# One transformer-like block on one core: the order of the first Strassen period and the way the first norm's gain reaches the core

## Chip, cores and metric

The kernel runs on 1 core of one Trainium2 chip. The metric is the device time of one execution in microseconds (us); the median of 3 runs of the kernel before is 1046.34 us (1046.23 to 1046.36).

## What is computed

One layer of a streaming encoder in float32, for 512 tokens of width 1024: a SwiGLU feed-forward (hidden width 2816) with half a residual, a mixer (chunked attention beside a convolution module, both gated), and a second SwiGLU feed-forward, each between two RMS norms.

```python
def rms_norm(x, g):
    y = x * lax.rsqrt(jnp.mean(x * x, axis=-1, keepdims=True) + EPS)
    return y * g

def swiglu(x, w_gate, w_up, w_down):
    return (jax.nn.silu(x @ w_gate) * (x @ w_up)) @ w_down

h = x
f = swiglu(rms_norm(h, ffn1_norm_pre), ffn1_w_gate, ffn1_w_up, ffn1_w_down)
h = h + 0.5 * rms_norm(f, ffn1_norm_post)
h = h + rms_norm(hybrid_mixer(rms_norm(h, mix_norm_pre), ...), mix_norm_post)
f = swiglu(rms_norm(h, ffn2_norm_pre), ffn2_w_gate, ffn2_w_up, ffn2_w_down)
h = h + 0.5 * rms_norm(f, ffn2_norm_post)
```

## The kernel before

Every product is made in float32 from two reduced-precision parts (`fp32r`) of each operand: a high part, which ScalarE (ACT) casts, and a low part, the rest, which VectorE (DVE) subtracts. `mm3` (lines 129 to 133) then issues three products to TensorE (PE): high by high, high by low, low by high.

**The start.** SP loads four tiles of `x` (128 tokens by 1024, 512 KB each) and weight blocks (`raw`, 512 KB each). The gain of the first norm has 1024 numbers; lines 268 to 271 load it with two DMAs of 256 KB, each of which writes the same 512 numbers to all 128 partitions. Meanwhile TensorE transposes the identity `WARM` times into a bank that nobody reads (lines 274 to 276). `stats1` sums squares on ACT and takes the root on GpSimd (POOL); `scaled1` (line 545) multiplies half a row of `h` by the root and the gain on DVE; `quarter` (line 558) transposes what came out on TensorE and ACT casts it into `uh`, the high part of the first feed-forward's input. On ACT the cast of the first weight block, `whi` (line 92), is written ahead of the four casts of `uh` (line 566). The first product is the matmul of line 196.

**The seven products.** Blocks 0 to 2 of the 22 hidden blocks of a feed-forward are made the plain way, blocks 3 to 21 (`CLASSIC = 3`) by Strassen's scheme, Winograd's form: seven half-size products in place of eight. The token sums s1 to s4 are made once; for each block j, four sums of weights are made on DVE: T1 and T3 in one tile `t13` (`sums13`, line 342), T2 and T4 in `t24` (`sums24`, line 349), T2 from T1. `parts(j, n)` makes the high part on ACT (line 363) and the low part on DVE (line 367) of the operand n: "b" (the gate block itself), "t13", "t24", "b22". `periods` (line 424) goes over j. In period j TensorE makes `first_products(j)` (b, t13 and t24, first halves), `third_products(j-1)` and `second_products(j)` (b and t13, second halves), 84 matmuls of 256 columns in all, while DVE and ACT prepare the operands of block j+1. Two small additions take products out of PSUM: `first_sum(j)` (line 417, a copy on ACT, of the first product's bank) and `second_sum(j)` (line 421, an addition on DVE, of the bank of the third of the first products). `second_products(j)` goes on accumulating in these two banks.

The feed-forward runs under `in_order()`, that is, each of TensorE, DVE and ACT works in the order in which the code is written. For the first period (j == j0, which is 3), `first_sum` and `second_sum` stand right behind `first_products` (lines 436 to 438), ahead of everything that prepares block 4. In later periods they stand between these steps. Tiles: `xn` (`wide`) has 3 buffers, `raw` 3, the pairs `whi`/`wlo` 6, PSUM 8 banks.

Of the kernel before, what the change touches and what calls it, by code (L numbers as in the profile page):

```python
# [8 lines left out]
F32 = mybir.dt.float32  # L9
# [3 lines left out]
ALU = mybir.AluOpType  # L13

P = 128
S = 512
D = 1024
# [21 lines left out]
C_ALL = C_LNB + NC  # L39

TAIL = 5
WARM = 36
AHEAD = 3
HALF = S // 2
CLASSIC = 3
# [7 lines left out]
def kernel(  # L53
# [11 lines left out]
    nc = tc.nc  # L65
# [4 lines left out]
    gpool = ctx.enter_context(tc.tile_pool(name="gpool", bufs=2))  # L70
# [9 lines left out]
    def bank():  # L80
        return psum.tile([P, 512], F32, name="ps")

    def two_banks():
        return [bank(), bank()]

    def wide():

        return tmps.tile([P, D], F32, name="xn")
# [17 lines left out]
    def pair_tiles():  # L106
        return ring.tile([P, 1024], F32R, name="whi"), ring.tile([P, 1024], F32R, name="wlo")
# [145 lines left out]
    ident = const.tile([P, P], F32, name="ident")  # L253
    make_identity(nc, ident)
    h = const.tile([P, NT, D], F32, name="h")
# [6 lines left out]
    def load_x(t):  # L262
        nc.sync.dma_start(out=h[:, t, :], in_=x[t * P:(t + 1) * P, :])

    load_x(0)
    load_x(1)

    g_first = gpool.tile([P, D], F32, name="gain")
    for b in range(2):
        sl = slice(b * 512, (b + 1) * 512)  # L270
        nc.sync.dma_start(out=g_first[:, sl], in_=gains[0, sl].partition_broadcast(P))
    with tc.manual_schedule(engines={mybir.EngineType.PE}):

        warm = bank()
        for _ in range(WARM):
            nc.tensor.transpose(warm[:, 0:P], ident, ident)
    ch = const.tile([P, C_ALL], F32, name="ch")
    tab_d = dram.tile([H, TABP], F32, name="tab_d")
# [44 lines left out]
    def seven_products(u, sums, hid, gu, j0, acts):  # L323
# [4 lines left out]
        s1, s2, s3, s4, _ = sums  # L328
# [9 lines left out]
        def add(out, a, b, op=ALU.add):  # L338
            nc.vector.tensor_tensor(out=out, in0=a, in1=b, op=op)  # L339
# [9 lines left out]
        def sums24(j):  # L349
            gate, up = raw[j]  # L350
            t24 = gu.tile([P, 1024], F32, name="t24")
            add(t24[:, lo], up[:, hi], ops[j]["t13"][1][:, lo], op=ALU.subtract)
            add(t24[:, hi], gate[:, hi], t24[:, lo], op=ALU.subtract)
            b22 = [gu.tile([P, 512], F32R, name=f"b22{p}", bufs=2) for p in "hl"]
            ops[j] |= {"t24": (pair_tiles(), t24), "b22": (b22, up[:, hi])}

        def parts(j, n):
            high(j, n)
            low(j, n)

        def high(j, n):
            (h_, _), src = ops[j][n]
            nc.scalar.copy(out=h_, in_=src)  # L363
# [53 lines left out]
        def first_sum(j):  # L417
            xs[j] = wide()
            nc.scalar.copy(out=xs[j][:, q[0]], in_=g[j][0][:, q[0]])

        def second_sum(j):
            add(xs[j][:, q[1]], g[j][1][:, q[0]], xs[j][:, q[0]])

        def periods():
            for j in range(j0, NF + 1):
                p, n = j - 1, j + 1
                old, now, new = p >= j0, j < NF, n < NF
                if old:
                    x, (g1, g2, g3) = xs[p], g[p]
                    y = ys[p] = wide()  # L430
                    add(x[:, q[2]], g2[:, q[0]], x[:, q[0]])
                    add(y[:, q[3]], g3[:, q[0]], x[:, q[2]])
                    silu(y[:, q[0]], g1[:, q[0]])
                if now:
                    first_products(j)
                if j == j0:
                    first_sum(j)
                    second_sum(j)
                if new:
                    sums13(n)  # L440
                    parts(n, "b")
                elif now:
                    prefetch(1)
                if now and j > j0:
                    first_sum(j)
                if new:
                    parts(n, "t13")
                elif now:
                    prefetch(2)
                if now and j > j0:  # L450
                    second_sum(j)
                if new:
                    sums24(n)
                if old:
                    third_products(p)
                    add(x[:, q[3]], g2[:, q[0]], x[:, q[0]])
                if new:
                    parts(n, "t24")
                elif now:
                    down_parts(2)  # L460
                if old:
                    silu(y[:, q[1]], x[:, q[3]])
                    add(y[:, q[2]], g3[:, q[0]], x[:, q[1]])
                    nc.vector.tensor_tensor(out=hid[:, p, :], in0=y[:, lo], in1=y[:, hi], op=ALU.mult)  # L464
                if new:
                    parts(n, "b22")
                load(j + 2)
                if now:
                    second_products(j)
# [75 lines left out]
    def scaled1(t, b):  # L545
        xn, r = xns[t]
        sl = slice(b * 512, (b + 1) * 512)
        nc.vector.scalar_tensor_tensor(xn[:, sl], h[:, t, sl], r, g_first[:, sl], op0=ALU.mult, op1=ALU.mult)

    def pre1(t):  # L550
        stats1(t)
# [475 lines left out]
```

## Time and profile before

| | |
|---|---|
| median of 3 runs | 1046.34 us (1046.23 to 1046.36) |
| the profiled execution, its own time | 1046.96 us |
| span in its profile | 1045.1 us |
| TensorE busy | 1030.9 us (99%) |
| DVE busy | 772.9 us (74%) |
| ACT busy | 476.0 us (46%) |
| mean granted clock of TensorE | 0.997 of full speed |

A busy time is the sum over an engine's instructions. Matmuls overlap: one of 256 columns is shown with 283 ns, and the next starts 120 ns behind it. What TensorE loses is therefore read from its idle times and from the distance of starts.

### The profile page before, as it was taken

What the parts mean: (1) busy time and instruction counts of PE and PEld (TensorE: products, weight loads), DVE (VectorE), ACT (ScalarE), POOL (GpSimd) and SP (SyncE); (2) the same over time, 40 slices, a digit from 0 to 9 for tenths busy, and PEclk for the clock granted to TensorE, in tenths of its full rate; (3) what the DMA queues carried; (4) which work ended last, traced back from release to release, by engine and by line L of the source; (5) the groups of instructions that cost most, each with busy time, mean ns of one, the idle gap of its engine ahead of it and who ended that gap; (6) DMA issues with size and microseconds to landing.
All of it is one profiled execution on the core that took longest, in us unless ns stands there. A gap on an engine that the chain in (4) does not pass through costs nothing.

```text
span 1045.1 us, 16111 instructions
## 1 busy us (share of the span) xinstructions
PE 1030.9 (99%) x6540; PEld 938.4 (90%) x6540; DVE 772.9 (74%) x1187; ACT 476.0 (46%) x785; POOL 20.7 (2%) x42
## 2 busy tenths in 40 slices
PE   8999999999999999999999999999999999999997
PEld 7999999998888898888888888899999999988886
DVE  6988898987332559999969776488889898963314
ACT  6434444445232432677874444354444444442311
POOL 1000000000000100000000100010000000000000
PEclk9999999999999999999999999999999999999999
DMA  7233333336323133333221145131334333452302
GB/s 245 64 100 110 101 114 102 101 102 220 101 88 96 41 112 109 121 96 97 82 87 61 41 132 169 43 101 41 103 101 121 100 104 102 127 177 88 95 20 81
DMA packets 30330, 106.92 MB, mean 102 GB/s; under 512 B 3488, under 2 KB 4136, under 8 KB 30256
## 3 DMA queue, kind: packets, MB, share of 16 engines
q1 hardware_dynamic: 27936, 100.94, 30.5%
q10 hardware_dynamic: 2320, 4.96, 1.5%
q8 instruction: 51, 0.84, 0.3%
q14 instruction: 23, 0.19, 0.1%
HBM read 103.77 MB, written 2.12 MB: 101 GB/s over the span
## 4 chain that ended last, share of the span: by engine, by line
PE 84%; DVE 12%; ACT 2%; DMA 1%; issue 1%; SPq 0%; DVEq 0%; POOLq 0%; ACTq 0%
PE ps L214 27%; PE ps L131 16%; PE ps L133 16%; PE ps L132 16%; DVE wlo L367 5%; PE ps L196 4%; DVE t L339 4%; ACT whi L363 1%; DVE xn L339 1%; DMA raw<-in_w 1%; PE ps L826 1%; PE ps L809 1%; PE ps L176 1%; DVE hid L464 1%; DVE b22l L367 1%
## 5 line engine op out<-in xcount | busy, mean ns | idle before, releaser
L131 PE MATMUL ps<-uh,whi 128*128 128x256 f32 (+1 forms) x808 | 255.6, 316 | 0.1
L133 PE MATMUL ps<-uh,wlo 128*128 128x256 f32 (+1 forms) x808 | 253.1, 313 | 0.0
L132 PE MATMUL ps<-ul,whi 128*128 128x256 f32 (+1 forms) x808 | 252.8, 313 | 0.0
L93 DVE TENSOR_TENSOR wlo<-raw,whi 128x1024 fp32r<-128x1024 f32 x108 | 131.5, 1220 | 134.3 <-ACT whi L92 132.0
L92 ACT CAST whi<-raw 128x1024 fp32r<-128x1024 f32 x108 | 112.8, 1051 | 167.6 <-PE ps L214 128.3
L214 PE MATMUL ps<-whi,act 128*128 128x512 f32 x640 | 172.7, 389 | 0.0
L133 PEld LDWEIGHTS ps<-uh,wlo 128*128 128x128 f32 x808 | 154.3, 191 | 9.1
L363 ACT CAST whi<-t 128x1024 fp32r<-128x1024 f32 x76 | 79.8, 1050 | 180.4 <-DVE t L339 169.4
L131 PEld LDWEIGHTS ps<-uh,whi 128*128 128x128 f32 x808 | 154.4, 191 | 8.2 <-DVE xn L339 0.3
L132 PEld LDWEIGHTS ps<-ul,whi 128*128 128x128 f32 x808 | 154.5, 191 | 8.0
L214 PEld LDWEIGHTS ps<-whi,act 128*128 128x128 f32 x640 | 120.0, 188 | 24.8
L367 DVE TENSOR_TENSOR wlo<-t,whi 128x1024 fp32r<-128x1024 f32 x76 | 93.1, 1225 | 31.6 <-ACT whi L363 31.5
L214 PE MATMUL ps<-wlo,act 128*128 128x512 f32 x320 | 99.4, 389 | 0.0
L637 DVE SCALAR_TENSOR_TENSOR acc<-c,ch,acc 128x512 f32<-128x512 f32 x120 | 86.1, 746 | 1.5
L339 DVE TENSOR_TENSOR xn<-ps,xn 128x256 f32<-128x256 f32 x190 | 79.4, 419 | 6.8 <-PE ps L133 5.5
L214 PEld LDWEIGHTS ps<-wlo,act 128*128 128x128 f32 x320 | 60.1, 188 | 12.5
L339 DVE TENSOR_TENSOR t<-raw,t 128x512 f32<-128x512 f32 x76 | 52.2, 687 | 1.3
L339 DVE TENSOR_TENSOR t<-raw 128x512 f32<-128x512 f32 x76 | 48.8, 683 | 0.2 <-DMA raw<-in_w 0.2
L367 DVE TENSOR_TENSOR wlo<-raw,whi 128x1024 fp32r<-128x1024 f32 x38 | 46.3, 1218 | 0.0
L133 PE MATMUL ps<-s2h,wlo 128*128 128x256 f32 x152 | 43.6, 287 | 1.5 <-DVE wlo L367 1.5
L131 PE MATMUL ps<-s2h,whi 128*128 128x256 f32 x152 | 43.5, 287 | 1.4 <-ACT whi L363 1.4
L131 PE MATMUL ps<-gain,whi 128*128 128x256 f32 x152 | 43.5, 286 | 0.0
(198 smaller groups left out, 1902.9 us busy)
## 6 DMA issues: line engine op xcount, KB each, us to landing
raw<-in_w SPq DMA_DIRECT2D x132, 512.0 KB, 3.6
raw<-in_wm SPq DMA_DIRECT2D x52, 512.0 KB, 3.6
gain<-in_gains ACTq DMA_DIRECT2D x5, 512.0 KB, 4.3
h<-in_x SPq DMA_DIRECT2D x4, 512.0 KB, 9.6
out<-h SPq DMA_DIRECT2D x3, 512.0 KB, 2.6
bias<-tab_d ACTq DMA_DIRECT2D x8, 128.0 KB, 3.5
bias<-tab_d ACTq DMA_DIRECT2D x8, 112.0 KB, 2.8
gain<-in_gains SPq DMA_DIRECT2D x2, 256.0 KB, 7.2
```

What stands on the lines that cost most here:

```text
L92: nc.scalar.copy(out=hi, in_=src)
L93: nc.vector.tensor_tensor(out=lo, in0=src, in1=hi.bitcast(F32), op=ALU.subtract)
L131: nc.tensor.matmul(ps, a[0], b[0], start=start, stop=False, **kw)
L132: nc.tensor.matmul(ps, a[0], b[1], start=False, stop=False, **kw)
L133: nc.tensor.matmul(ps, a[1], b[0], start=False, stop=stop, **kw)
L176: nc.tensor.transpose(pss[k // 4][:, (k % 4) * P:(k % 4 + 1) * P], xn[:, k * P:(k + 1) * P], ident)
L196: nc.tensor.matmul(ps[:, lo:hi], w[wi][:, k * P:(k + 1) * P], u[ui][:, k, lo:hi], start=i == 0 and k == 0, stop=i == 2 and k == KD - 1)
L214: nc.tensor.matmul(acc[n], a[ai], w[bi][:, n * 512:(n + 1) * 512], start=start and i == 0, stop=stop and i == 2)
L339: nc.vector.tensor_tensor(out=out, in0=a, in1=b, op=op)
L363: nc.scalar.copy(out=h_, in_=src)
L367: nc.vector.tensor_tensor(out=l_, in0=src, in1=h_.bitcast(F32), op=ALU.subtract)
L637: nc.vector.scalar_tensor_tensor(acc[:, j, :], cs[j][:, w:w + S], wc, acc[:, j, :], op0=ALU.mult, op1=ALU.add)
```

## The change

At the start: one DMA on ACT's queue loads the gain's 4 KB into one partition (`row`, a buffer of `xn`); after 16 warm-up transposes instead of 36, two float32 matmuls with a column of ones spread it over 128 partitions into two banks of PSUM, and three more transposes follow. `scaled1` reads the gain from PSUM. SP's two gain DMAs are gone.

In the first period: `sums13` and the parts of "b" stand ahead of `first_sum` and `second_sum`, and `sums24` ahead of the parts of "t13". Later periods are written as before.

```diff
-WARM = 36
+WARM = 16
...
+    row = wide()
+    nc.scalar.dma_start(out=row[0:1, :], in_=gains[0:1, :])
     load_x(0)
     load_x(1)
-
-    g_first = gpool.tile([P, D], F32, name="gain")
-    for b in range(2):
-        sl = slice(b * 512, (b + 1) * 512)
-        nc.sync.dma_start(out=g_first[:, sl], in_=gains[0, sl].partition_broadcast(P))
...
+        ones = wp.tile([1, P], F32, name="ones")
+        nc.vector.memset(ones, 1.0)
         warm = bank()
         for _ in range(WARM):
+            nc.tensor.transpose(warm[:, 0:P], ident, ident)
+
+        g_first = two_banks()
+        for b, ps in enumerate(g_first):
+            nc.tensor.matmul(ps, ones, row[0:1, b * 512:(b + 1) * 512], start=True, stop=True)
+        for _ in range(3):
             nc.tensor.transpose(warm[:, 0:P], ident, ident)
...
                 if now:
                     first_products(j)
-                if j == j0:
-                    first_sum(j)
-                    second_sum(j)
                 if new:
                     sums13(n)
                     parts(n, "b")
                 elif now:
                     prefetch(1)
-                if now and j > j0:
+                if now:
                     first_sum(j)
-                if new:
+
+                if j == j0:
+                    second_sum(j)
+                    sums24(n)
                     parts(n, "t13")
+                elif new:
+                    parts(n, "t13")
+                    second_sum(j)
+                    sums24(n)
                 elif now:
                     prefetch(2)
-                if now and j > j0:
                     second_sum(j)
-                if new:
-                    sums24(n)
...
-        nc.vector.scalar_tensor_tensor(xn[:, sl], h[:, t, sl], r, g_first[:, sl], op0=ALU.mult, op1=ALU.mult)
+        nc.vector.scalar_tensor_tensor(xn[:, sl], h[:, t, sl], r, g_first[b], op0=ALU.mult, op1=ALU.mult)
```

TensorE's order at the start of the program (the difference; `ident` is the identity, `ones` the column of ones, the first `xn` the buffer with the gain's row):

```order
-L276 MATMUL ps<-ident 128x128 x36
-L563 MATMUL ps<-ident,xn 128x128 x16
+L275 MATMUL ps<-ident 128x128 x16
+L279 MATMUL ps<-xn,ones 128x512 x2
+L281 MATMUL ps<-ident 128x128 x3
+L569 MATMUL ps<-ident,xn 128x128 x16
 L196 MATMUL ps<-uh,whi 128x256 x8
```

Two matmuls of 512 columns and three transposes stand where the last 20 transposes stood.

DVE's order in the first period of the first feed-forward, before (b22l_520 belongs to block 3; t13, t24, the wlo and b22l_659 to block 4; the first row of xn is `second_sum(3)`):

```order
L367 TENSOR_TENSOR b22l_520<-raw_503,b22h_519 128x512
L339 TENSOR_TENSOR xn_641<-ps_603,xn_641 128x256
L339 TENSOR_TENSOR t13_644<-raw_600,raw_598 128x512
L339 TENSOR_TENSOR t13_644<-raw_600 128x512
L367 TENSOR_TENSOR wlo_648<-raw_598,whi_647 128x1024
L367 TENSOR_TENSOR wlo_650<-t13_644,whi_649 128x1024
L339 TENSOR_TENSOR t24_655<-raw_600,t13_644 128x512
L339 TENSOR_TENSOR t24_655<-raw_598,t24_655 128x512
L367 TENSOR_TENSOR wlo_661<-t24_655,whi_660 128x1024
L367 TENSOR_TENSOR b22l_659<-raw_600,b22h_658 128x512
```

And in the change, the same piece:

```order
L372 TENSOR_TENSOR b22l_512<-raw_495,b22h_511 128x512
L344 TENSOR_TENSOR t13_633<-raw_592,raw_590 128x512
L344 TENSOR_TENSOR t13_633<-raw_592 128x512
L372 TENSOR_TENSOR wlo_637<-raw_590,whi_636 128x1024
L344 TENSOR_TENSOR xn_642<-ps_595,xn_642 128x256
L344 TENSOR_TENSOR t24_645<-raw_592,t13_633 128x512
L344 TENSOR_TENSOR t24_645<-raw_590,t24_645 128x512
L372 TENSOR_TENSOR wlo_639<-t13_633,whi_638 128x1024
L372 TENSOR_TENSOR wlo_651<-t24_645,whi_650 128x1024
L372 TENSOR_TENSOR b22l_649<-raw_592,b22h_648 128x512
```

`second_sum(3)` moved behind three instructions, and both halves of t24 moved ahead of t13's low part. On ACT the cast of "b" moved ahead of the copy `first_sum(3)`. The same holds for the second feed-forward. TensorE's products stand in the same order in the periods.

## Rows read from the trace of the kernel before

**Rows 1.** The page, busy time of each engine
```profile
PE 1030.9 (99%) x6540; PEld 938.4 (90%) x6540; DVE 772.9 (74%) x1187; ACT 476.0 (46%) x785; POOL 20.7 (2%) x42
```

**Rows 2.** Waits of TensorE over the whole span: total us, times, longest
```profile
PE ps L563 <- DVE xn L548: 2.0, 2, 1.6
PE ps L133 <- DVE wlo L367: 1.5, 2, 0.8
PE ps L131 <- ACT whi L363: 1.4, 2, 0.7
```

**Rows 3.** Timeline of the start: start us, duration, engine, line, instruction [idle before <-releaser]
```profile
6.02 0.57 POOL L159 TENSOR_TENSOR rstd<-ms,mhalf 128x1 f32<-128x1 f32 x1
...
8.33 0.75 DVE L548 SCALAR_TENSOR_TENSOR xn<-h,rstd,gain 128x512 f32<-128x512 f32 x1 [7.48 <-DMA gain<-in_gains]
...
9.34 2.08 DVE L548 SCALAR_TENSOR_TENSOR xn<-h,rstd,gain 128x512 f32<-128x512 f32 x3 [0.25 <-DMA gain<-in_gains]
...
10.62 1.05 ACT L92 CAST whi<-raw 128x1024 fp32r<-128x1024 f32 x1 [3.73 <-DMA raw<-in_w]
11.58 2.04 ACT L566 CAST uh<-ps 128x512 fp32r<-128x512 f32 x4
...
13.18 0.99 PE L196 MATMUL ps<-uh,whi 128*128 128x256 f32 x6 [1.06 <-ACT uh L566]
```

**Rows 4.** Stretches at the start: length, busy PE, PEld, DVE, ACT, POOL; PEclk, DMA, GB/s
```profile
4.50:5.00 0.50, 0.50 (x4) 0.50 (x3) 0.00 (x0) 0.50 (x1) 0.00 (x0) 1.00 1.07 377
...
6.00:6.50 0.50, 0.50 (x8) 0.50 (x5) 0.00 (x0) 0.50 (x1) 0.48 (x1) 1.00 0.70 156
```

**Rows 5.** DMA issues by queue: count, size, median us from issue to landing
```profile
gain<-in_gains SPq DMA_DIRECT2D x2, 256.0 KB, 7.2
...
ch<-in_chan ACTq DMA_DIRECT2D x1, 80.0 KB, 1.9
```

**Rows 6.** Timeline of DVE, first period of the first feed-forward
```profile
50.24 0.68 DVE L367 TENSOR_TENSOR b22l<-raw,b22h 128x512 fp32r<-128x512 f32 x1
53.54 0.42 DVE L339 TENSOR_TENSOR xn<-ps,xn 128x256 f32<-128x256 f32 x1 [2.62 <-PE ps L133]
53.88 1.28 DVE L339 TENSOR_TENSOR t<-raw 128x512 f32<-128x512 f32 x2
55.08 1.22 DVE L367 TENSOR_TENSOR wlo<-raw,whi 128x1024 fp32r<-128x1024 f32 x1
...
57.42 1.41 DVE L339 TENSOR_TENSOR t<-raw,t 128x512 f32<-128x512 f32 x2
59.95 1.23 DVE L367 TENSOR_TENSOR wlo<-t,whi 128x1024 fp32r<-128x1024 f32 x1 [1.11 <-ACT whi L363]
```

**Rows 7.** Timeline of ACT, the same period
```profile
50.65 0.37 ACT L419 COPY xn<-ps 128x256 f32<-128x256 f32 x1 [2.07 <-PE ps L133]
```

**Rows 8.** Timeline of TensorE, first feed-forward, start of the second period
```profile
58.96 0.28 PE L133 MATMUL ps<-s1h,wlo 128*128 128x256 f32 x1
59.97 0.39 PE L131 MATMUL ps<-s2h,whi 128*128 128x256 f32 x1 [0.72 <-ACT whi L363]
...
61.45 0.28 PE L131 MATMUL ps<-s2h,whi 128*128 128x256 f32 x1
```

**Rows 9.** Timeline of DVE, first period of the second feed-forward
```profile
725.97 0.69 DVE L367 TENSOR_TENSOR b22l<-raw,b22h 128x512 fp32r<-128x512 f32 x1
```

**Rows 10.** Timeline of TensorE, second feed-forward, first and second period
```profile
729.22 0.28 PE L131 MATMUL ps<-gain,whi 128*128 128x256 f32 x1
...
733.48 0.28 PE L133 MATMUL ps<-s1h,wlo 128*128 128x256 f32 x1
...
739.61 0.28 PE L131 MATMUL ps<-uh,whi 128*128 128x256 f32 x1
```

**Rows 11.** Stretches of the second feed-forward, TensorE alone: length, busy; PEclk, DMA, GB/s
```profile
736.00:738.00 2.00, 2.00 (x11) 0.51 0.41 61
738.00:740.00 2.00, 2.00 (x14) 0.64 0.52 207
```

More of the change, by code (lines that the diff above doesn't have):

```diff
@@ L263, in load_x @@
         nc.sync.dma_start(out=h[:, t, :], in_=x[t * P:(t + 1) * P, :])
+    row = wide()
+    nc.scalar.dma_start(out=row[0:1, :], in_=gains[0:1, :])
     load_x(0)
     load_x(1)
-    g_first = gpool.tile([P, D], F32, name="gain")
-    for b in range(2):
-        sl = slice(b * 512, (b + 1) * 512)
-        nc.sync.dma_start(out=g_first[:, sl], in_=gains[0, sl].partition_broadcast(P))
-    with tc.manual_schedule(engines={mybir.EngineType.PE}):
+    with tc.tile_pool(name="warm", bufs=1) as wp, tc.manual_schedule(engines={mybir.EngineType.PE}):
+        ones = wp.tile([1, P], F32, name="ones")
+        nc.vector.memset(ones, 1.0)
         warm = bank()
         for _ in range(WARM):
+            nc.tensor.transpose(warm[:, 0:P], ident, ident)
[3 more added lines that the diff above has]
+        for _ in range(3):
             nc.tensor.transpose(warm[:, 0:P], ident, ident)
```

## Prediction

> **What bounds the kernel.** I read the page's busy times first: TensorE is busy 1030.9 us of 1045.1 [rows 1], so only its idle time and its clock can give anything. The waits of TensorE come next. The three largest that the change can touch are a wait at the first transposes (2.0 us) and two kinds of wait, twice each, for the low and the high part of a weight operand in the periods [rows 2]. Each of these operand waits comes once per feed-forward, and the timeline shows where: at the start of period 4, before the products with t24 [rows 8, 10]. In all other periods TensorE waits for neither, so DVE and ACT keep up there. Three places count, then: the start and two first periods.
>
> A measurement of this kernel can tell about 0.2% (2.1 us) from no change.
>
> **The start.** DVE's first scaling of h starts at 8.33 and ends an idle time that the gain's DMA ended, while the root for this tile was done at 6.02 + 0.57 = 6.59 [rows 3]. The two gain DMAs land 7.2 us after their issue [rows 5]. With the gain there in time, the four scalings (0.69 us apart, 2.08 for the last three [rows 3]) would run from 6.65 to 9.4 in place of 11.4: 2.0 us earlier on DVE. The operand's place changes from SBUF to PSUM; I cost that at nothing.
>
> ACT is the second chain. The cast of the first weight block waits for its DMA until 10.62, the four casts of uh stand behind it, 0.5 us apart, and the first product starts at 13.18, behind the third of them [rows 3]. An earlier gain is worth nothing if the weight block still comes at 10.6. But the gain DMAs stand ahead of it on SP's queue and are 0.52 MB. The DMA engines moved 377 GB/s at 4.5 to 5.0 us and 156 GB/s at 6.0 to 6.5, when the gain was under way [rows 4]. At 377 GB/s the 0.52 MB alone are 1.4 us; if three us of the slow rate go to the full one, another 1.4 us are won. So the block comes 1.4 to 2.8 us earlier, at 7.8 to 9.2; I take 8.3. Then the cast ends at 9.35, the third cast of uh at 10.9, and the first product starts 2.3 us earlier. All later loads of x and weights move by the same bytes, so what follows moves with it.
>
> What is added must be hidden. The gain's row is a DMA of 4 KB on ACT's own queue. Nearest rows: 80 KB on this queue landed in 1.9 us, with little beside it; the two 256 KB gains took 7.2 us beside x [rows 5]. I take about 3 us, near the small one, so it lands near 3.8 us. The 16 transposes, 4 per half us there [rows 4], end about 3.3 us. The two float32 matmuls of 512 columns have no row. Four transposes of 128 columns are 0.5 us at that rate, a lower bound of 1 us for the pair; the second half is wanted by the second scaling at 6.65 + 0.7 = 7.35, so the cover is 7.35 - 3.8 = 3.5 us, and they may cost three times as much before anything waits for them. I cost them at nothing and keep a late row, 7.9 us, for the range: then scaling starts near 9 and the start loses 0.7 us. The Trainium skill, "FP8 and Floating Point Precision", TensorE Precision Notes, says that true float32 takes four passes through the array. By it the pair would be an estimated 4 us at that rate and end at 7.8, 0.45 us late, and the start would gain 1.85 us in place of 2.3; no row here shows such a matmul, and my sum does not use it. The DMA's issue on ACT stands ahead of work that waits for x anyway. The start: 2.3 us, between -0.7 and 2.9.
>
> **First feed-forward.** DVE ends b22l of block 3 near 50.9 and idles 2.62 us for the bank of the third product [rows 6]; t13, the low part of b, t13's low part and t24 all queue behind it, so that t24's low part ends at 61.2. In the change, T1 and T3 start at 50.85 (1.20 us, from the distance of rows), the low part of b follows (1.22, to 53.3), and then second_sum finds its bank full at 53.54, as before. T2 and T4 take 1.33 to 55.2, the two low parts 1.2 each, to 57.6. ACT's cast of b now stands ahead of the copy at 50.65 [rows 7]; ACT idles 2.07 us there, and a cast is 1.05, so it fits. TensorE wants t24's parts at 59.1 and 59.3: 1.7 us to spare. What goes: 58.96 to 61.45 are four starts, at 0.12 us each 0.48 [rows 8], so 2.49 - 0.48 = 2.0 us. (0.12 is the distance from 729.22 to 733.48, 35 starts [rows 10].)
>
> **Second feed-forward.** From 733.48 to 739.61 are 22 starts [rows 10]: 6.13 - 22 x 0.12 = 3.5 us lost. It is more than in the first because here the granted clock fell behind the wait, to 0.51 and 0.64 of full speed for the two stretches of 2 us [rows 11], that is the lower level of 1.2 GHz for some 3.4 us. With no wait there is no reason for the fall. DVE is later here against TensorE: b22l starts at 725.97 [rows 9], so T1, T3 and the low part of b end at 726.6 + 1.2 + 1.2 = 729.0, and second_sum ends at 729.4. TensorE's product into that bank starts at 729.22 [rows 10]: a new wait of 0.25 us, as price of putting the sum behind three instructions. t24's low part ends at 733.1 against 733.8 wanted: it holds by 0.7 us. Net 3.25 us.
>
> **Sum.** 2.3 + 2.0 + 3.25 = 7.55 us. The profiled execution took 1046.96 us, which gives 1039.4; it stands 0.6 above the median of the runs, and against the median the result is **1038.8 us**. DMAs that the earlier t24 frees (raw buffers) start earlier; the queue has room.
>
> **Rivals.**
> 1. *The start gives nothing.* The row lands late beside the megabyte of x, or the matmuls with one row are long, or the clock is at its lower level when the first products begin. For: 17 of the 36 transposes are gone, and their distance halves only near 5 us (4 and 8 per half us [rows 4]; the granted clock reads 1.00 in both rows, so the rate is the better witness). Against: between 7.5 and 13.2 us TensorE did little but 16 transposes and the products still began at 0.12 us. At the lower level for 3.4 us the second feed-forward lost 1.5 us beyond the 2.0 of its waits. The start then gives -0.7 to 0.8: 1040.3 to 1041.8 us. The Trainium skill, "TensorE: Matmul & The Clock Gate", Part 1, says that the array begins at the lower level and is let up by sustained work; by that rule this rival is to be expected if the row leaves a gap.
> 2. *The second feed-forward gives its waits alone.* If the timed runs do not have the fall of the clock, or if the new wait brings one, 1.5 us are missing: 1040.3 us. For: such a fall came in one of the two feed-forwards with nearly the same wait. Against: the three runs agree within 0.13 us and lie near the profiled one.
> 3. *The waits only move.* The work of DVE is the same; if the high part of t24 still comes late, because ACT's casts queue behind the copy, only the start is left: 1044 us. Against: ACT idles there. This is also the case in which the change does not do what it says.
> 4. *Slower.* The clock stays at the lower level from the start on. A us there costs 0.44 us (1.5 of 3.4), so the kernel is slower than before by over 0.2% only from (7.55 + 2.1)/0.44 = 22 us of products at that level, 1048.4 us or more. For: less warm-up. Against: after the second feed-forward's wait it was back after some 3.4 us of products.
>
> **Chances and range.** Forecast 0.65, rival 1 0.15, rival 2 0.11, rival 3 0.06, rival 4 0.03. The range runs from all three places at their best (2.9 + 2.0 + 3.5, with half a us for small waits beside: 1037.4) to rival 1 at its worst, 1041.8. Rival 3 lies at the bound and gives 0.01 to faster and 0.05 to no change. So faster 0.92, same 0.05, slower 0.03.
>
> **What would show it.** Right: the first scaling starts near 6.7 and reads PSUM with no DMA behind its idle time; the cast of the first weight block starts at 7.8 to 9.2; the first product at 10.3 to 11.3; no wait of TensorE for t24 in either period 4; granted clock 1.00 around 735; a wait of some 0.25 us at the product into second_sum's bank in the second feed-forward. Wrong: products at 0.21 us distance behind the start; a weight block that still lands near 10.6; a fall of the clock elsewhere; a wait for t24 one period later.

## The result and the profile after

| | before | after |
|---|---|---|
| median | 1046.35 us (1046.23 to 1046.37, 4 runs) | 1039.46 us (1038.58 to 1040.70, 4 runs) |
| ratio after to before | | 0.9935 (0.9918 to 0.9952) |
| the profiled execution, its own time | 1046.96 us | 1038.58 us |
| its span | 1045.1 us | 1036.5 us |

The change is faster by 6.9 us; 1038.8 was forecast, in a range of 1037.4 to 1041.8. The four runs lie in two pairs, 1038.58 twice and 1040.34 and 1040.70. The profiled execution is of the lower pair, so the 8.4 us by which it is faster than the profiled one before are more than the medians show; the experiments ask what the other pair is.

The page of the changed kernel, busy times [rows 1]; behind them its chain of waits by engine:

```profile
PE 1028.9 (99%) x6527; PEld 936.1 (90%) x6527; DVE 773.0 (75%) x1188; ACT 476.0 (46%) x785; POOL 20.3 (2%) x42
...
PE 97%; DVE 2%; ACT 1%; issue 0%; DVEq 0%; POOLq 0%; POOL 0%; ACTq 0%
```

The same chain was 84% TensorE and 12% DVE before. The waits of TensorE, which had three kinds that the change could touch [rows 2], are down to one that stood there before as well, for the identity:

```profile
PE ps L275 <- POOL ident masks.py:199: 1.3, 1, 1.3
```

**The start.** Its timeline, the rows that answer to [rows 3]:

```profile
4.95 2.14 PE L279 MATMUL ps<-xn,ones 1*128 1x512 f32 x4
6.08 0.57 POOL L159 TENSOR_TENSOR rstd<-ms,mhalf 128x1 f32<-128x1 f32 x1
6.68 2.72 DVE L554 SCALAR_TENSOR_TENSOR xn<-h,rstd,ps 128x512 f32<-128x512 f32 x4 [5.68 <-POOL rstd L159]
...
7.49 3.29 PE L569 MATMUL ps<-ident,xn 128*128 128x128 f32 x16
7.62 1.05 ACT L92 CAST whi<-raw 128x1024 fp32r<-128x1024 f32 x1 [0.66 <-DMA raw<-in_w]
...
10.60 1.90 PE L196 MATMUL ps<-uh,whi 128*128 128x256 f32 x8
...
12.33 1.11 PE L196 MATMUL ps<-uh,wlo 128*128 128x256 f32 x8
```

The first scaling now waits for the root alone; the cast of the first weight block starts at 7.62 in place of 10.62, and the first product at 10.60 in place of 13.18. But the first eight products take 12.33 - 10.60 = 1.73 us, 0.216 each, where the products of the kernel before start 0.12 apart. The stretches of the start, in the columns of [rows 4], tell why:

```profile
6.00:6.50 0.50, 0.50 (x2) 0.18 (x1) 0.00 (x0) 0.50 (x1) 0.42 (x1) 1.00 0.96 385
...
8.50:9.00 0.50, 0.50 (x4) 0.26 (x3) 0.50 (x2) 0.50 (x2) 0.00 (x0) 0.73 0.98 401
9.00:10.00 1.00, 1.00 (x6) 1.00 (x6) 1.00 (x2) 0.69 (x3) 0.00 (x0) 0.50 1.01 414
...
12.00:13.00 1.00, 1.00 (x10) 1.00 (x9) 1.00 (x3) 1.00 (x2) 0.00 (x0) 0.93 0.76 246
```

The DMA engines move 385 GB/s at 6.0 to 6.5 us, where the gain's broadcast had held them at 156. And TensorE's granted clock falls to 0.50 of full speed, the level of 1.2 GHz, near 8.7 us and is back only past 12: most of the transposes of the normed rows and the first products run at that level.

**The first periods.** DVE in the first feed-forward [rows 6], then the copy on ACT [rows 7]:

```profile
48.52 1.29 DVE L344 TENSOR_TENSOR t<-raw 128x512 f32<-128x512 f32 x2
49.72 1.22 DVE L372 TENSOR_TENSOR wlo<-raw,whi 128x1024 fp32r<-128x1024 f32 x1
51.62 0.42 DVE L344 TENSOR_TENSOR xn<-ps,xn 128x256 f32<-128x256 f32 x1 [0.68 <-PE ps L133]
51.96 1.41 DVE L344 TENSOR_TENSOR t<-raw,t 128x512 f32<-128x512 f32 x2
53.29 2.42 DVE L372 TENSOR_TENSOR wlo<-t,whi 128x1024 fp32r<-128x1024 f32 x2
...
48.73 0.37 ACT L424 COPY xn<-ps 128x256 f32<-128x256 f32 x1 [1.56 <-PE ps L133]
```

The idle time of 2.62 us on DVE is 0.68, and t24's low part is done at 53.29 + 2.42 = 55.71; TensorE wants it near 57.4. TensorE in the second feed-forward, at the product into `second_sum`'s bank [rows 10]:

```profile
724.09 0.28 PE L133 MATMUL ps<-uh,wlo 128*128 128x256 f32 x1
724.37 0.39 PE L131 MATMUL ps<-gain,whi 128*128 128x256 f32 x1
724.59 0.28 PE L132 MATMUL ps<-gain,whi 128*128 128x256 f32 x1
```

And two stretches of TensorE behind it [rows 11]:

```profile
736.00:738.00 2.00, 2.00 (x19) 1.00 0.59 223
738.00:740.00 2.00, 2.00 (x19) 1.00 0.36 35
```

The new wait is there: the two distances are 0.28 and 0.22 in place of 0.12 each, 0.26 us together. The fall of the clock to 0.51 and 0.64 is gone in this execution.

**Where the 8.6 us of span went.** The first product with s1h of each period of Strassen's scheme is a good mark. It comes at 50.39 and 232.14 us (first and last of the first feed-forward) and 724.90 and 907.00 (second) before, and at 48.47, 227.03, 719.89 and 898.70 after.

| stretch | before | after | won | forecast |
|---|---|---|---|---|
| start, up to the first mark | 50.39 | 48.47 | 1.92 | 2.3 |
| first feed-forward, first to last mark | 181.75 | 178.56 | 3.19 | 2.0 |
| between (mixer) | 492.76 | 492.86 | -0.10 | 0 |
| second feed-forward | 182.10 | 178.81 | 3.29 | 3.25 |
| behind the last mark | 138.1 | 137.8 | 0.3 | 0 |

Of the 3.19 us the second mark to the third (57.64 to 69.71 before, 55.67 to 65.75 after) has 1.99; 1.15 come one by one in the periods behind it, where nothing was forecast. They are small waits like this one of the kernel before, with distances of 0.32 and 0.22 us where 0.12 is usual:

```profile
107.03 0.28 PE L133 MATMUL ps<-uh,wlo 128*128 128x256 f32 x1
107.35 0.38 PE L131 MATMUL ps<-gain,whi 128*128 128x256 f32 x1
107.57 0.28 PE L132 MATMUL ps<-gain,whi 128*128 128x256 f32 x1
```

After, all single products between the first and the last mark of the first feed-forward stand at their 0.12 us. Why DVE can cause such waits in any period shows in its own timeline, at the low part of t24 in two periods that follow each other; two rows of the kernel before, then two of the change:

```profile
109.79 1.23 DVE L367 TENSOR_TENSOR wlo<-t,whi 128x1024 fp32r<-128x1024 f32 x1 [0.84 <-ACT whi L363]
119.92 1.23 DVE L367 TENSOR_TENSOR wlo<-t,whi 128x1024 fp32r<-128x1024 f32 x1 [0.83 <-ACT whi L363]
...
104.01 1.23 DVE L372 TENSOR_TENSOR wlo<-t,whi 128x1024 fp32r<-128x1024 f32 x1 [0.83 <-ACT whi L368]
114.14 1.23 DVE L372 TENSOR_TENSOR wlo<-t,whi 128x1024 fp32r<-128x1024 f32 x1 [0.83 <-ACT whi L368]
```

DVE needs 10.12 to 10.13 us for a period in both kernels (9.07 busy, 0.83 of waiting for ACT's cast of t24), and TensorE 84 x 0.12 = 10.08. So DVE falls behind by 0.04 to 0.05 us in each period, and what it has in hand behind the first period decides when TensorE has to wait. In period 5 of the first feed-forward t24's low part ends 1.1 us before its product starts in the kernel before, and 2.7 us before it in the change. The 16 periods that follow take some 0.7 us from this.

### The profile page after: what moved, and what is told of

Same layout as the page of the kernel before. It is cut to its first block, busy times and chain, and to the rows that moved or that the text cites. A ratio compares the mean times of both kernels' runs of the same rounds, so it can differ in the third digit from the quotient of the medians.

```text
span 1036.5 us, 16089 instructions
## 1 busy us (share of the span) xinstructions
PE 1028.9 (99%) x6527; PEld 936.1 (90%) x6527; DVE 773.0 (75%) x1188; ACT 476.0 (46%) x785; POOL 20.3 (2%) x42
## 4 chain that ended last, share of the span: by engine, by line
PE 97%; DVE 2%; ACT 1%; issue 0%; DVEq 0%; POOLq 0%; POOL 0%; ACTq 0%
PE ps L214 27%; PE ps L131 20%; PE ps L133 20%; PE ps L132 20%; PE ps L196 5%; PE ps L176 1%; PE ps L832 1%; PE ps L815 1%; DVE acc L643 1%; PE ps L805 0%; PE ps L804 0%; PE ps L275 0%; DVE ptl L93 0%; PE ps L569 0%; DVE wlo L93 0%
## 5 line engine op out<-in xcount | busy, mean ns | idle before, releaser
L131 PE MATMUL ps<-s1h,whi 128*128 128x256 f32 x152 | 43.0, 283 | 0.0
L132 PE MATMUL ps<-s1l,whi 128*128 128x256 f32 x152 | 43.0, 283 | 0.0
```

Of the source, the lines that this page charges most:

```text
L131: nc.tensor.matmul(ps, a[0], b[0], start=start, stop=False, **kw)
L132: nc.tensor.matmul(ps, a[0], b[1], start=False, stop=False, **kw)
```

## The experiments

The theory is that the three places give their terms independently of each other. The first rival is that the start is worth little, because the clock is at its lower level when the first products begin. Later runs ask what splits the change's times into two, and what the order in the first period has to be. "Start only" and "periods only" split the change. Each group of runs has its own runs of the kernel before beside it: 1046.12, 1046.11, 1046.12 and 1046.02 us.

### The change again

No edit.

> The changed kernel once more, to see how far its executions lie apart (1038.58 to 1040.7 in four, against 0.14 us for the kernel before). Theory: the spread comes from the start. [...] Expected: 1038.5 to 1041 us, apart by over 1 us; the profiled execution shows the lower level between 8 and 16 us. Rival: the spread comes from the periods, which have no wait left; then the start looks alike in every trace and a fall of the clock or waits show up elsewhere.

1039.44 us (1038.24 to 1040.79, 6 runs), ratio 0.9935 (0.9924 to 0.9947). Three runs are at 1038.2 to 1038.4, three at 1040.5 to 1040.8: the two groups are the kernel's own. The profiled execution, 1038.32 us, in the timeline of TensorE:

```profile
4.55 1.98 PE L279 MATMUL ps<-xn,ones 1*128 1x512 f32 x4
...
10.90 1.57 PE L196 MATMUL ps<-uh,whi 128*128 128x256 f32 x8
```

And in two stretches of TensorE (length, busy; PEclk, DMA, GB/s):

```profile
7.00:8.00 1.00, 0.58 (x4) 0.74 1.04 426
8.00:9.00 1.00, 1.00 (x7) 0.50 1.01 414
```

Here the clock fell more than a us sooner, near 7.5, and rose sooner, near 10.9, so that the eight products took 1.57 us in place of 1.90: when the fall comes differs from execution to execution of one kernel.

### Start only: the new start with the old order in the first period

```diff
                 if now:
                     first_products(j)
+                if j == j0:
+                    first_sum(j)
+                    second_sum(j)
                 if new:
                     sums13(n)
                     parts(n, "b")
```

(and the lines behind as before the change.)

> The new start with the old first period. Theory: the start alone gives between 0 and 2.5 us (2.6 earlier at the first product, 0.8 or more given back at the lower clock level): 1044 to 1046.4 us, with a spread of over 1 us, and the waits of the periods (3.75 us in the first feed-forward, 3.6 in the second) as before, but the fall of the clock in the second feed-forward may come or not, since the wait now lies elsewhere in time (1.5 us). Rival (spread from the periods): runs within 0.2 us.

1045.19 us (1043.17 to 1046.67, 11 runs), ratio 0.999 (0.9982 to 0.9999): 0.9 us of the 2.3. The profiled execution has its first mark at 48.19, 2.2 us sooner than before, with the clock at 0.50 from 8 to 11 us. Its first feed-forward, however, takes 182.11 us against 181.75, for the clock falls there too (stretches of TensorE):

```profile
58.00:60.00 2.00, 1.24 (x7) 0.79 0.70 254
60.00:62.00 2.00, 2.00 (x11) 0.50 0.63 190
```

In the recorded execution of the kernel before the same stretches read 1.00 and 1.00. So this wait comes with the fall in some executions and not in others. The fall costs 13.57 - 12.07 = 1.5 us between the second mark and the third, as the prediction had it for the second feed-forward. But the whole first feed-forward is only 0.36 us longer, because all later periods here take 10.08 us: the small waits of the kernel before are missing, with the old order and an early start. While TensorE ran at the lower level DVE caught up, and t24's low part ends 2.7 us ahead of its product in period 5, as in the change. The kernel before spreads as well, from 1045.11 to 1048.3 in 17 runs.

### Periods only: the old start with the new order

```diff
-WARM = 16
+WARM = 36
...
+    g_first = gpool.tile([P, D], F32, name="gain")
+    for b in range(2):
+        sl = slice(b * 512, (b + 1) * 512)
+        nc.sync.dma_start(out=g_first[:, sl], in_=gains[0, sl].partition_broadcast(P))
```

(against the change; `row`, `ones`, their matmuls and the three transposes behind them go, and `scaled1` reads the gain as before.)

> The old start with the new first period. Theory: 2.0 us in the first feed-forward's first period, some 1.1 us of small waits in its later periods (DVE no longer trails), 3.3 us in the second feed-forward: 1046.35 - 6.4 = 1039.9 us, runs within 0.3 us, no wait of TensorE in the later periods. Rival: the small waits went away because of the earlier start; then waits of 0.04 to 0.3 us per period stay in the first feed-forward and the time is near 1041.

1039.83 us (1039.72 to 1040.34, 5 runs), ratio 0.9937 (0.9925 to 0.9949): 6.3 us, where the terms of the two periods were 5.25. The marks give the feed-forwards 178.57 and 178.81 us, as in the change; the 1.15 us of small waits are gone without the new start. Two things follow. On the median the start is worth 1039.83 - 1039.44 = 0.4 us: 1.5 in the change's lower group, -0.7 in its upper one. And without the first period's waits the runs lie within 0.6 us: the two groups of the change come with the new start.

### Row early: 8 transposes ahead of the row's products, 16 behind

```diff
-WARM = 16
+WARM = 8
...
-        for _ in range(3):
+        for _ in range(16):
             nc.tensor.transpose(warm[:, 0:P], ident, ident)
```

> The change with 8 transposes ahead of the two row matmuls and 16 behind them (16 and 3 in the change), so that real work stands directly ahead of the first products and the row matmuls come as early as the row lands. Theory: the clock does not fall at 8.7 us, the first products run at 0.12 us distance from near 10.6 us, and the time is 0.8 to 2 us below the change's, near 1037.8, with a spread under 0.5 us. Rival: the clock falls because there is less warm-up in all; then it falls here too, since the sum of work is about the same, and the time is as the change's. The start of the first row matmul (4.95 us in the change, directly behind the transposes) shows whether the row lands before 4.9.

1040.34 us (1039.98 to 1040.56, 5 runs), ratio 0.9941 (0.9929 to 0.9953). It was to keep the clock up, and did the opposite (timeline):

```profile
3.24 3.78 PE L279 MATMUL ps<-xn,ones 1*128 1x512 f32 x4
...
6.95 3.68 PE L281 MATMUL ps<-ident 128*128 128x128 f32 x16
...
13.13 1.00 PE L196 MATMUL ps<-uh,whi 128*128 128x256 f32 x6 [0.31 <-ACT uh L572]
```

The row had landed by 3.24 us. The pair takes 3.78 us here and 1.98 in the execution above: the two levels of the clock. The transposes behind it, too, are at the lower level, 3.68 us for 16, and push the first product to 13.13: the old start's time, with a total 0.5 us above that of "periods only".

### Split row: the row in two reduced-precision parts

```diff
...
         for b, ps in enumerate(g_first):
-            nc.tensor.matmul(ps, ones, row[0:1, b * 512:(b + 1) * 512], start=True, stop=True)
-        for _ in range(3):
+            sl = slice(b * 512, (b + 1) * 512)
+            split(row_h[:, sl], row_l[:, sl], row[0:1, sl])
+            nc.tensor.matmul(ps, ones_r, row_h[:, sl], start=True, stop=False)
+            nc.tensor.matmul(ps, ones_r, row_l[:, sl], start=False, stop=True)
+        for _ in range(8):
```

(`split` casts the high part on ACT and subtracts the low part on DVE; the lines that make the new tiles are left out.)

> The change with a cheaper spread of the gain: the row is split on ACT and DVE into a high and a low part of reduced precision, four matmuls of 512 columns in place of two in float32, and 8 transposes behind. Theory: the two float32 matmuls take four passes each (pair 2.0 us at full clock, 3.8 us at the lower level, as the two traces of the change and of the early row show), and whether they meet the full clock decides between executions of 1038.3 and of 1040.6 us. Four single passes are half of it, 0.9 us at full clock, 1.7 at the lower level, done before the root at 6.6 us in either case. Expected: one group of times, 1037.5 to 1038.5 us, apart by under 1 us. Rival: two groups as before, since the falling clock and not the length of the matmuls decides.

1038.42 us (1036.86 to 1039.38, 5 runs), ratio 0.9925 (0.9912 to 0.9937). The profiled execution, 1036.86 us, in the timeline of TensorE:

```profile
4.59 0.49 PE L285 MATMUL ps<-row_h,ones_r 1*128 1x512 f32 x1
...
5.39 0.39 PE L286 MATMUL ps<-row_l,ones_r 1*128 1x512 f32 x1
...
9.98 1.40 PE L196 MATMUL ps<-uh,whi 128*128 128x256 f32 x8
```

One stretch of TensorE:

```profile
9.00:10.00 1.00, 0.98 (x8) 1.00 1.00 410
```

Four products take 5.39 + 0.39 - 4.59 = 1.19 us in place of 1.98, the clock stays at 1.00, and the first mark comes at 47.37, 3.0 us sooner than before. But the five runs still spread by 2.5 us: it is better on the median, and does not always come out so. One group within 1 us was expected, so the spread does not come from the length of the float32 pair alone. Nor does a fall of the clock explain three of the four slower runs: they list a mean granted clock of 0.999, and the profiled one, which had no fall at the start, 0.998.

### Sum earlier: both sums right behind T1 and T3

Old start, as in "periods only", and in the first period (`high` is the part on ACT, `low` the part on DVE; `sums24` still stands ahead of the parts of "t13"):

```diff
                 if new:
                     sums13(n)
-                    parts(n, "b")
+                    high(n, "b")
+                    if j == j0:
+                        first_sum(j)
+                        second_sum(j)
+                    low(n, "b")
```

> The old start and the new first period, but with both sums directly behind T1 and T3, ahead of b's low part. Theory: in the second feed-forward the product into the bank that the sum on DVE reads waits 0.26 us in the change (0.16 us and a longer restart), because three instructions stand ahead of the sum; with two ahead it waits for nothing, and b's low part is still in time: 1039.8 - 0.25 = 1039.55 us and no such wait. Rival: b's low part or t24's becomes late in the first feed-forward, where DVE waits for the bank until 53.5 us: a wait of up to 1 us at the start of the second period, 1040 us or more.

1040.92 us (1040.74 to 1041.24, 5 runs), ratio 0.9952 (0.9938 to 0.9965): 1.1 us slower than "periods only". DVE in the first and the second feed-forward:

```profile
53.07 0.42 DVE L339 TENSOR_TENSOR xn<-ps,xn 128x256 f32<-128x256 f32 x1 [1.40 <-PE ps L133]
...
725.16 0.42 DVE L339 TENSOR_TENSOR xn<-ps,xn 128x256 f32<-128x256 f32 x1 [0.18 <-PE ps L133]
```

The new wait of TensorE in the second feed-forward is gone, as it should be. But DVE idles 1.40 us in the first, and small waits are back: the first feed-forward takes 179.15 us by the marks against 178.57, the second 178.84 against 178.81, so that nothing is left of the wait that went. The marks account for 0.6 of the 1.1 us. The small waits start late, in the twelfth or thirteenth distance of marks of each feed-forward, and this fits the 0.04 to 0.05 us by which DVE falls behind per period: t24's low part is 1.5 us ahead of its product in period 5 of both feed-forwards, between the 1.1 of the kernel before, which waits from the sixth distance on, and the 2.7 of the change, which doesn't wait. So the unforecast 1.15 us are of this kind.

### Traffic: the change with the two old gain DMAs kept, into a tile that nobody reads

```diff
     load_x(1)
+    g_unused = gpool.tile([P, D], F32, name="gain")
+    for b in range(2):
+        sl = slice(b * 512, (b + 1) * 512)
+        nc.sync.dma_start(out=g_unused[:, sl], in_=gains[0, sl].partition_broadcast(P))
```

> The change with the two old gain DMAs still issued on SP's queue, into a tile that nobody reads. Theory: half of the start's gain hangs on the weight block, which waits behind these 0.52 MB; it lands near 10.5 us again, its cast on ACT holds the casts of uh, and the first product starts near 13.1 us: the start gives nothing even when the clock is up, 1039.8 to 1040.8 us. Rival: the scalings alone set the start; then the first product comes near 10.9 us as in the change, and two groups of times, 1038.3 and 1040.6, stay.

1042.83 us (1041.45 to 1043.24, 5 runs), ratio 0.9965 (0.9953 to 0.9978): 3.4 us slower than the change, more than expected. The timeline of DVE, ACT and TensorE:

```profile
6.54 2.72 DVE L558 SCALAR_TENSOR_TENSOR xn<-h,rstd,ps 128x512 f32<-128x512 f32 x4 [5.54 <-POOL rstd L159]
10.69 1.05 ACT L92 CAST whi<-raw 128x1024 fp32r<-128x1024 f32 x1 [3.89 <-DMA raw<-in_w]
...
13.25 1.23 PE L196 MATMUL ps<-uh,whi 128*128 128x256 f32 x8 [2.41 <-ACT uh L576]
```

And stretches of TensorE:

```profile
6.00:6.50 0.50, 0.50 (x2) 1.00 0.83 152
...
15.00:16.00 1.00, 1.00 (x7) 0.50 0.64 262
```

The scalings start at 6.54 all the same, and gain nothing: the weight block behind the broadcast comes at 10.69 as before, the first product at 13.25, and 152 GB/s are back. So the gain of the start hangs on the broadcast ahead of the weights on SP's queue, and an early gain alone is worth nothing; whether an earlier block alone would be worth something was not run. What is over the expectation goes with a second fall of the clock, at 14.4 to 17.8 us, in the recorded execution: from the first product to the first mark it takes 38.71 us against 37.21 in the kernel before.

### Warm 24: 24 transposes ahead of the row's products

`WARM = 24` in place of 16.

> The change with 24 warm-up transposes ahead of the row matmuls (16 in the change, 36 before). Theory: the executions near 1040.6 are those in which the clock was not yet up when the row matmuls began (4.6 to 4.95 us), so that the pair took 3.8 us and the first scalings waited. 24 transposes last to about 6 us, past the rise; then the pair takes 2.0 us in all executions, ends near 8 us, the second scaling is late by some 0.7 us, and all times lie near 1039, apart by under 1 us. Rival: two groups 2 us apart stay, so the groups come from the fall of the clock behind the row matmuls.

1039.51 us (1038.28 to 1040.06, 5 runs), ratio 0.9934 (0.9922 to 0.9947). In the profiled execution, 1038.28 us, the clock read 1.00 up to the first product at 10.84, with the pair at 1.98 us, and there was no fall at the start; its first mark comes at 48.21, against 48.29 to 48.47 in the recorded executions of the change. The five runs still spread by 1.8 us, where under 1 was expected. More transposes alone leave the median where it was, and neither the theory nor the rival came out as written.

### Filled: split row, 12 transposes behind it and 2 behind each group of four

```diff
-        for _ in range(8):
+        for _ in range(12):
             nc.tensor.transpose(warm[:, 0:P], ident, ident)
...
             nc.tensor.transpose(ps[:, k * P:(k + 1) * P], xns[t][0][:, c0:c0 + P], ident)
+        for _ in range(2):
+            nc.tensor.transpose(warm[:, 0:P], ident, ident)
```

> The change with the row split in two parts of reduced precision (four single-pass matmuls), 12 transposes behind them and 2 idle transposes behind each of the four quarters. Theory: what still spreads the times with the split row (1036.9 to 1039.4) is a fall of the clock in the stretch of the quarters, in which TensorE does 16 transposes in 2.6 us; with the gaps filled it stays up in all executions and the first product starts near 10 us at 0.12 us distance: 1036.9 to 1037.5 us, apart by under 0.7 us, the fastest of all. Rival: the filling transposes delay the quarters' casts by more than they save: near 1038 with a narrow spread; or the spread has another cause and stays at 2 us.

1037.24 us (1036.93 to 1039.1, 5 runs), ratio 0.992 (0.9907 to 0.9934); four of the five lie at 1036.9 to 1037.4. Stretches of TensorE of the profiled execution:

```profile
7.00:8.00 1.00, 1.00 (x11) 1.00 1.02 418
```

The first product stands at 9.99 and the first mark at 47.36. This is the best kernel of the study: 9 us faster than before and 2.6 us faster than the change beside it. The fifth run is not explained. That the filled gaps keep the clock up, as expected, is not shown either: the split row's recorded execution had no fall at the start without them.

### As later: the first period in the order of the later ones

Old start; the special order for j0 is dropped.

```diff
-                if j == j0:
-                    second_sum(j)
-                    sums24(n)
-                    parts(n, "t13")
-                elif new:
+                if new:
                     parts(n, "t13")
                     second_sum(j)
                     sums24(n)
```

> The old start, and the first period written as the later ones: b's low part, then the copy, t13's low part, then the sum on DVE, then T2 and T4. Theory: the sum stands behind four instructions; in the first feed-forward it costs near 0.2 us, in the second the product into its bank at 729 waits some 1.4 us, and DVE, kept back, stays behind by some 0.05 us per period: 1039.8 + 0.2 + 1.4 + up to 2 = 1041.4 to 1043.4 us. Rival: T2 and T4 ahead of t13's low part are not needed; then the time is 1039.8 to 1040.2 as with the change's order.

1041.71 us (1041.6 to 1041.8, 5 runs), ratio 0.9959 (0.9946 to 0.9971): 1.9 us slower than "periods only". TensorE in the second feed-forward:

```profile
727.81 0.39 PE L131 MATMUL ps<-gain,whi 128*128 128x256 f32 x1 [1.20 <-DVE xn L339]
```

One more low part ahead of `second_sum` makes the wait of 0.16 us one of 1.20, and the second feed-forward 180.02 us long against 178.81. The place of `second_sum` is right to about one instruction: earlier, DVE idles; later, TensorE does. T2 and T4 stand behind t13's low part here, and no wait for t24 came of it (10.08 us from the second mark to the third in both feed-forwards). That part of the change is not shown to be needed.

### The change once more

No edit; beside "filled" and "as later".

> The changed kernel beside the two others on the same chip: two groups of times near 1038.4 and 1040.6 us, as before.

1039.84 us (1038.2 to 1040.33, 5 runs), ratio 0.9937 (0.9924 to 0.9949): two runs at 1038.2 and 1038.4, three at 1039.8 to 1040.3. The mean clocks listed with the runs say that the upper ones are not all alike: these three list 0.996, while one of the upper runs of each earlier set (1040.34 and 1040.49) lists 0.999; the three recorded executions, all with a fall at the start, list 0.997 to 0.998.

### Warm 11: 11 transposes ahead, so that the row's products run at the lower level

`WARM = 11` in place of 16.

> The change with 11 warm-up transposes in place of 16 and nothing else: they end at 3.7 us, ahead of the rise of the clock that the other traces show between 4.6 and 5 us. Theory: the group of the change's executions near 1040.5 us are those in which the clock is not yet up when the row matmuls begin; here that is so in all of them, so all times lie in one group at 1040 to 1041 us, and the trace shows the pair taking some 3.7 us from 3.7 on, slow transposes and a first product near 12 to 13 us. Rival: the groups come from something else (when DMAs land, where the clock falls later); then two groups 2 us apart stay, or the pair is fast from 4.8 us on and the times are those of the fast group, 1038.3 us.

1039.73 us (1039.11 to 1039.83, 5 runs), ratio 0.9938 (0.9924 to 0.9952). Timeline:

```profile
3.89 3.78 PE L279 MATMUL ps<-xn,ones 1*128 1x512 f32 x4
...
7.71 2.07 DVE L554 SCALAR_TENSOR_TENSOR xn<-h,rstd,ps 128x512 f32<-128x512 f32 x3 [0.26 <-PE ps L279]
...
11.73 1.77 PE L196 MATMUL ps<-uh,whi 128*128 128x256 f32 x8
```

The pair at the lower level ends at 7.67, behind the time at which the second scaling wants it, and the products start at 11.73 and at half rate. The runs are one group, as expected, but 0.3 us below the expected range and 0.7 us better than the change's upper group in "the change again". So a start at the lower level gives times of nearly that kind, by the way seen here. That the change's upper group is this very case isn't shown: all of its recorded executions were of the lower group. One thing speaks for it: the time at which the clock comes up varies. The 36 transposes of the old start took 5.70 us in "periods only", 6.19 in the kernel before, 6.84 in "as later" and 6.98 in "sum earlier". A rise as late as in the last two, near 7 us, would leave the change's pair at the lower level for most of its length. It can hardly be the only case: a listed clock of 0.996 is below that of every recorded execution with the new first period that had no fall at the start (0.998 to 0.999).

## Why the prediction was right, and where it was not

**The total** is 0.7 us from the median and within the range, but two of its terms were wrong, in opposite directions: the start gave 1.9 us less on the median, and small waits that the sum didn't have gave 1.15 more. That the two nearly cancel is luck.

**First feed-forward, 2.0 us:** right for the first period, by the mechanism forecast; 1.99 between the second mark and the third. The order on DVE came as written; the new idle time at `second_sum` is 0.68 us, where 0.2 was implied.

**Second feed-forward, 3.5 less 0.25:** right in both parts. The distance of the second and third mark (732.15 to 745.72 before, 727.35 to 737.42 after) shrank by 3.50, the clock reads 1.00 around 737, and the new wait is 0.26. Rival 3 falls with it, and rival 2 for the execution recorded. But its price was wrong: where the old first period runs without a fall, small waits come in the place of the 1.5 us, and by the first feed-forward of "start only" the two cases are 0.36 us apart.

**"In all other periods TensorE waits for neither":** this step failed. It rested on the view of waits, in which the two operands appear twice each; the small waits of the later periods are of 0.02 to 0.23 us and were visible only in the distances of starts. They were 1.15 us in the first feed-forward. DVE does not keep up: it needs 10.12 us for a period against TensorE's 10.08, in every run recorded (single periods 10.2 to 10.4). The 74% are its mean over the whole span; in the periods it is 90% busy and waits for ACT most of the rest. It lives on what it has in hand behind the first period, and the old order left it too little there (1.1 us by t24's low part). "Periods only" has the waits gone with the old start, "sum earlier" brings a part of them back, and in "start only" and the second feed-forward of the kernel before the fall of the clock gave DVE the time.

**The start, 2.3 us:** the mechanism was right, the size was not. First scaling at 6.68 (6.65 forecast), no DMA behind its idle time; cast of the weight block at 7.62 (8.3 taken), before the 7.8 to 9.2 given, for three us at 156 in place of 377 GB/s are 1.76 us and not the 1.4 of the sum; first product at 10.60 (10.3 to 11.3 given); "traffic" shows that the broadcast on the queue has to go for it. What failed is "I cost them at nothing", of the two float32 products. They take 1.98 us at the full level and 3.78 at the lower, against a lower bound of 1, and they start at 4.55 to 4.95, not at 3.8: the 16 transposes ahead of them start 0.21 us apart and end at 4.6 to 5.0, not at 3.3. (Four in a half-us stretch of [rows 4] counts also those that only reach into it.) In the recorded executions of the change the scalings still waited for the root alone; the cost came behind the pair, where the clock fell to 0.50 in all three of them. At the lower level the pair also makes the second scaling late, as "warm 11" shows. The sign of the wrong case, products at 0.21 us distance, stood in the list and came. With "periods only" as the base, the start gives 1.5 us in one group of executions and -0.7 in the other, 0.4 on the median. Rival 1 with its -0.7 to 0.8 describes about half of the executions (8 of 15), and deserved a chance near 0.5, not 0.15. Had the 1.15 us of small waits not come on top, the median would have been near 1040.6.

The Trainium skill, "FP8 and Floating Point Precision", TensorE Precision Notes, has true float32 at four passes; the estimate by it was 4 us at the lower rate. The row says 3.78: the page agrees, and it was a better guide to the pair's length than my bound from transposes. The Trainium skill, "TensorE: Matmul & The Clock Gate", Part 1, also has the array begin at the lower level, and says that how long it stays there differs between runs of one kernel. The traces agree with both: the early pairs of "row early" and "warm 11" took 3.78 us, and the pair of the change, at about the same time in each execution, took 2.14 us in one and 1.98 in two.

## What to carry to other kernels

In a pipeline in lock-step, compare the period of each engine alone with that of the engine that should set the pace, and not their mean busy shares. Where a helper is slower by as little as 0.04 us in 10, the first period is where it gets its lead: a wait there is paid again in small pieces, each too short for a list of waits, so compare the distances of like marks from period to period. Ask what else the queue carries ahead of the first weights: here two loads that broadcast 256 KB each put the first weight block 3 us back. And when work on the matmul engine takes the place of warm-up, its passes and its effect on the clock are terms of the sum: in two reduced-precision parts instead of float32 the same row took 0.8 us less, and the clock did not fall at the start in either of the two executions recorded.

## What the runs showed of the hardware that was not expected

In one execution of the change the clock fell with TensorE shown busy throughout (0.99 to 1.00 us of each us from 5 to 10 us), in the two others with 0.58 and 0.69 us busy from 7 to 8 us. In the old start it stayed up beside stretches that were nearly empty. Two stretches of TensorE in the kernel before:

```profile
8.00:9.00 1.00, 0.00 (x0) 1.00 0.88 352
...
12.00:13.00 1.00, 0.13 (x2) 1.00 1.03 418
```

Its products behind this began at 0.12 us. So the rows of busy time don't show why the clock fell here. It fell at 7.5 to 8.7 us in all five recorded executions with 16 transposes ahead of the float32 pair (three of the change, "start only", "traffic"). It did not fall at the start with 24 ahead ("warm 24"), with the pair wholly at the lower level ("row early", "warm 11") or with the split row, one or two executions each; what brings the fall was not settled. And at the start the granted clock reads 1.00 even where work runs at half rate ("row early": 1.00 in each stretch from 3 to 13 us, with the pair at 3.78 us): there the distance of like instructions is the witness.
